# Two of the four sums of weight blocks in the seven-product stage made by accumulating loads that GpSimd issues

## The chip, the cores and the metric

The kernel runs on one core of a Trainium2 chip. The metric is the device time of one execution in microseconds (us); the number quoted is the median of the runs shown. In views of the trace PE is TensorE, with its weight loads apart as PEld; DVE is VectorE, ACT is ScalarE, POOL is GpSimd, and SP is the engine that issues every DMA (a transfer between HBM, the chip's main memory, and the on-chip memory) of the kernel before.

## The reference, cut to what matters

Two layers of a transformer-like block run over 256 latent tokens and 256 context tokens. Everything is float32. The change lies in the first layer's feed-forward part, which both token streams go through with the same weights:

```python
def swiglu(h, w_up, w_down):
    gu = h @ w_up
    return (jax.nn.silu(gu[..., :FFN_HIDDEN]) * gu[..., FFN_HIDDEN:]) @ w_down
```

`h` has 1024 features and `FFN_HIDDEN` is 2816, so `w_up` has 22 pairs of column tiles of 128: a gate tile and an up tile each.

## The kernel before, in words

**A recorded plan.** The kernel does not issue its instructions as it is written. A recorder, `Plan`, collects all operations with the tiles that they read and write. `place` hands out buffers: tiles of one class share a fixed number of slots, given out in the order in which they came free. Class `raw` has 7 slots (4 KB for each of 128 partitions) and takes weights as they come from HBM, and sums of them; `whi` and `wlo` have 3 slots each. `order` then runs a list scheduler with a cost for each operation (`cost`), a latency for each engine, and a port that certain VectorE and GpSimd operations share (`shares`); `emit` issues the operations in that order, so every row of the trace has the line of `emit`, 313. Each engine then works through its own queue in order, and waits at an instruction whose inputs are not there.

**Split matmuls.** A float32 product is made of three float32r matmuls. A weight tile is split first: ScalarE rounds it into `hi` (`whi<-raw`), VectorE subtracts that from the original into `lo` (`wlo<-raw,whi`). The three products are hi*hi, hi*lo and lo*hi.

**The seven-product stage.** For 19 of the 22 hidden tiles of the first layer (j = 3 to 21), `up_seven` replaces the eight block products of a two-by-two block product (two halves of the 1024 features by gate and up) with seven, after Strassen and Winograd. A weight pair is four blocks of 128 x 512: b11 (gate, first half of the features), b21 (gate, second half), b12 (up, first half) and b22 (up, second half). The seven products use as weights b11 (called f1), b22 (f3), b21 (f2) and four sums:

```python
t1 = b11 + b12      t2 = t1 + b22      t3 = b12 + b22      t4 = t2 + b21
```

A call of `up_seven` loads two tiles of 512 KB, `raw[0]` = (b11, b22) and `raw[1]` = (b12, b21), and makes the sums on VectorE into two more `raw` tiles, `y` = (t1, t2) and `z` = (t3, t4), called `upy` and `upz` in the trace. Three tiles of 128 x 1024 are split: (f1, f3), (t1, t2), (t3, t4), and `f2` apart into a tile `wf`. Then TensorE runs the products in the order f1, t1, t2, f3, t3, f2, t4. Each is 12 matmuls of 256 columns, 84 in a call. Their right sides are tokens (`h` in the trace) or sums of tokens made earlier (`hs0` to `hs3`), so a row `up<-hs0h,whi` belongs to t1, `hs1` to t2, `hs2` to f3, `hs3` to t3, and `h,wf` to f2. The results gather in three PSUM banks (a, b, c) that are read between products:

```python
product(a, "f1", block(0, 0), True)
nc.scalar.activation(e[:, 0], a, AF.Copy)
product(c, "t1", sums[0], True)
nc.scalar.activation(f[:, 0], c, AF.Copy)
product(a, "t2", sums[1], False)
nc.scalar.activation(e[:, 1], a, AF.Copy)
product(c, "f3", sums[2], False)
```

So product t2, which adds to bank a, cannot start before ScalarE has copied a (`upe<-up`); t3 waits in the same way for the second copy. A tanh (`upf<-upe`, then `upe<-up`), two multiplications and a write to `hid` end a call. Between calls, `ada_step` puts in tiles of the conditioning vectors: a load `raw<-in_w_ada_t` and one or two passes `junkv<-raw,silb` on VectorE; in this stage one in every second call.

**What stands around the stage.** Ahead of it are the output projection (`pj`), two layer norms for each stream, whose inverse roots are taken by GpSimd (`rsp`, `rsn`, an instruction with `pow`), and the first three hidden tiles by eight products (`up_tile`). Behind it is the projection with `w_down` (`pj` again).

Of the kernel before, what the change touches and what calls it, by code (L numbers as in the profile page):

```python
# [10 lines left out]
F32 = mybir.dt.float32  # L11
F32R = mybir.dt.float32r
BF16 = mybir.dt.bfloat16
AF = mybir.ActivationFunctionType
ALU = mybir.AluOpType
# [114 lines left out]
class Plan:  # L130
# [29 lines left out]
    def cost(self, eng, method, args, kw, outs, ins):  # L160

        src = ins[0] if ins else outs[0]
        n = max(v.idx.size for v in (outs[0:1] or ins[0:1]))
        if eng == "tensor":
            if method == "transpose":
                return 0.109
            if kw["rhs"].tile.dt == F32R:
                return max(n, 256) * 0.4434e-3 + 0.0045
            return max(4 * n / 2400, 0.214)
        if eng == "scalar":  # L170
            c = src.idx.size / 1200 + (0.05 if src.tile.cls == "bank" else 0.093)
            c += 0.18 if isinstance(kw.get("scale"), View) else 0
            return c + (0.093 if kw.get("accum_out") is not None else 0)
        if eng == "vector":
            n = max(v.idx.size for v in (*outs[:1], *ins))
            wide = [v for v in ins if v.idx.size > 8]
            fast = (method in ("tensor_scalar", "tensor_copy") and len(wide) == 1
                    and wide[0].tile.cls != "bank")
            return n / (1920 if fast else 960) + 0.07
        if eng == "gpsimd":  # L180
            return n / 440 + 0.1 if n > 64 else 0.4 + 0.19 * max(0, n - 1)
        return max(0.35, 128 * n * 4 / 365e3)

    @staticmethod
    def shares(eng, ins):

        return eng == "gpsimd" or eng == "vector" and sum(v.tile.cls not in ("bank", "dram") for v in ins) >= 2

    def place(self):

# [45 lines left out]
    def order(self):  # L236
        n = len(self.ops)
# [14 lines left out]
        out = []  # L252
        port = 0.0
        warm, busy = False, 0.0
        while len(out) < n:
            best = None
            for e in self.ENGINES:
                t = clock[e]
                if not avail[e]:
                    if not future[e]:  # L260
                        continue
                    t = max(t, future[e][0][0])
                if best is None or t < best[0]:
                    best = (t, e)
            t, e = best
            while future[e] and future[e][0][0] <= t:
                heapq.heappush(avail[e], heapq.heappop(future[e])[1:])
            rank, i = avail[e][0]
# [17 lines left out]
            if self.shares(e, self.ops[i][5]):  # L286
                t = max(t, port)
# [3 lines left out]
            out.append(i)  # L291
            for u in users[i]:
                lat = 0.0 if self.ops[u][0] == e == "tensor" else self.LATENCY[e]
                if self.ops[u][0] == "tensor" and e != "tensor":
                    lat += 0.12
                ready[u] = max(ready[u], t + c + lat)
                waits[u] -= 1
                if not waits[u]:
                    heapq.heappush(future[self.ops[u][0]], (ready[u], self.rank[u], u))
# [25 lines left out]
class Builder:  # L325
# [681 lines left out]
    def up_seven(self, j, hT, S, dst):  # L1007

        nc, io = self.nc, self.io
        raw = [self.nc.tile("raw", [128, 2, 4, 128], F32, "raw") for _ in range(2)]  # L1010
        for i in range(2):
            nc.sync.dma_start(raw[i], io["w_up7"][j, i])
        f1, f3, b12, f2 = raw[0][:, 0], raw[0][:, 1], raw[1][:, 0], raw[1][:, 1]
        y = self.nc.tile("raw", [128, 2, 4, 128], F32, "upy")
        z = self.nc.tile("raw", [128, 2, 4, 128], F32, "upz")
        w = {}

        def part(src, names):
            hi = self.nc.tile("whi", [128, 2, 4, 128], F32R, "whi")
            lo = self.nc.tile("wlo", [128, 2, 4, 128], F32R, "wlo")  # L1020
            self.split_sbuf(HL(hi, lo), src)
            for i, n in enumerate(names):
                w[n] = HL(hi[:, i], lo[:, i])

        part(raw[0], ("f1", "f3"))
        nc.vector.tensor_tensor(y[:, 0], f1, b12, op=ALU.add)
        nc.vector.tensor_tensor(y[:, 1], y[:, 0], f3, op=ALU.add)
        part(y, ("t1", "t2"))
        nc.vector.tensor_tensor(z[:, 0], b12, f3, op=ALU.add)
        nc.vector.tensor_tensor(z[:, 1], y[:, 1], f2, op=ALU.add)  # L1030
        part(z, ("t3", "t4"))
        wf = self.a_tile([128, 2, 4, 128], F32R, "wf2")
        w["f2"] = HL(wf[:, 0], wf[:, 1])
        self.split_sbuf(w["f2"], f2)

        def block(kh, half):
            c = slice(half * 128, half * 128 + 128)
# [9 lines left out]
        e = self.s_tile([128, 2, 2, 128], "upe")  # L1047
# [430 lines left out]
def lay_out(inputs):  # L1478
# [3 lines left out]
    out = {}  # L1482
# [26 lines left out]
    up = g["w_up"].reshape(L, KD, 128, 2, KF, 128)  # L1509
    out["w_up"] = up.transpose(0, 4, 3, 2, 1, 5)  # L1510
    q = out["w_up"][0].reshape(KF, 2, 128, 2, 4, 128)
    out["w_up7"] = np.stack([np.stack([q[:, 0, :, 0], q[:, 1, :, 1]], axis=2),
                             np.stack([q[:, 1, :, 0], q[:, 0, :, 1]], axis=2)], axis=1)
    tok = g["w_up"][1].reshape(4, 2, 128, 2, FH)[..., :512]
    out["w_up_tok"] = tok.transpose(3, 0, 2, 1, 4)
    out["w_down"] = g["w_down"].reshape(L, KF, 128, D)
# [7 lines left out]
    t = np.arange(SEQ)  # L1524
    ph = lambda k: 2 * np.pi * ((t[:, None] * k[None, :]) % 256) / 256
    f1 = np.concatenate([np.cos(ph(np.arange(129))), np.sin(ph(np.arange(1, 128)))], axis=1)
# [34 lines left out]
```

## Time and profile before

| | |
|---|---|
| median of 3 runs | 1322.76 us (1322.4 to 1326.71) |
| the profiled execution | 1323.69 us |
| its span, first to last instruction | 1321.9 us |
| TensorE's granted clock, mean | 0.993 of full speed |
| TensorE busy | 1297.4 us, 98% |
| VectorE busy | 1000.4 us, 76% |
| ScalarE busy | 660.9 us, 50% |
| GpSimd busy | 102.4 us, 8% |
| moved by DMA | 214.27 MB, 162 GB/s over the span |

A busy TensorE is not TensorE at its peak: matmuls are pipelined, a row of the trace lasts longer than the distance to the next, and so distances between matmuls, not their durations, tell its pace. Stages are best read one by one, by windows of the span (in us from its start). Releasers of a wait are inferred from semaphores (counters by which one engine tells another that it is done).

### The profile page before, as it was taken

The numbers are of one execution on the slowest core, as the hardware profiler recorded it, in microseconds if no ns is written. First come the engines' busy times: TensorE is split into PE (matmuls) and PEld (weight loads), VectorE is DVE, ScalarE is ACT, GpSimd is POOL, SyncE is SP. The second block draws the span as 40 slices with busy tenths as digits, with TensorE's granted clock in tenths as the row PEclk, the third lists the DMA queues.
The fourth block names the chain that finished last, engine by engine and source line by source line (L and its number), as shares of the span: only waits on it lengthen the run. The fifth ranks groups of instructions, "written<-read, shape, count | busy, mean of one in ns | idle before, by whom it ended". The sixth has DMA issues, their size and how long they took to land.

```text
span 1321.9 us, 20368 instructions
## 1 busy us (share of the span) xinstructions
PE 1297.4 (98%) x7846; PEld 1145.6 (87%) x7846; DVE 1000.4 (76%) x1774; ACT 660.9 (50%) x1192; POOL 102.4 (8%) x99
## 2 busy tenths in 40 slices
PE   9999999999999999999999999989999999999997
PEld 8887888788888889999999888868789998799985
DVE  6988996675764787799999994677777758666665
ACT  4656675332222347555555433575865544544450
POOL 1032100000010111000000000142000101000000
PEclk8999999999999999999999999999999999999999
DMA  9633334344543840233435896043245874465551
GB/s 367 224 105 117 114 108 159 113 131 155 175 159 129 303 159 27 71 127 114 158 107 171 288 343 206 26 127 128 83 137 184 278 263 161 168 192 183 186 190 48
DMA packets 60817, 214.27 MB, mean 162 GB/s; under 512 B 7296, under 2 KB 8112, under 8 KB 60720
## 3 DMA queue, kind: packets, MB, share of 16 engines
q1 hardware_dynamic: 60720, 212.98, 47.9%
q8 instruction: 61, 1.00, 0.3%
q14 instruction: 36, 0.29, 0.1%
HBM read 211.88 MB, written 1.07 MB: 161 GB/s over the span
## 4 chain that ended last, share of the span: by engine, by line
PE 81%; DVE 11%; ACT 5%; issue 2%; POOL 1%; DMA 0%; SPq 0%; DVEq 0%; ACTq 0%; POOLq 0%
PE up L313 25%; PE pj L313 17%; PE gp L313 15%; PE bp L313 10%; PE zp L313 8%; DVE junkv L313 2%; ACT prob L313 2%; DVE wlo L313 1%; DVE mx L313 1%; PE ut L313 1%; ACT junka L313 1%; PE pvp L313 1%; DVE ptl L313 1%; DVE y L313 1%; DVE bst L313 1%
## 5 line engine op out<-in xcount | busy, mean ns | idle before, releaser
L313 DVE TENSOR_TENSOR wlo<-raw,whi 128x1024 fp32r<-128x1024 f32 x216 | 265.3, 1229 | 122.8 <-ACT whi L313 121.5
L313 ACT ACTIVATE whi<-raw 128x1024 fp32r<-128x1024 f32 x216 | 228.2, 1058 | 193.7 <-PE bp L313 71.3
L313 DVE SCALAR_TENSOR_TENSOR junkv<-raw,silb 128x1024 bf16<-128x1024 f32 x128 | 156.7, 1224 | 12.0 <-DMA raw<-in_w_ada_t 10.6
L313 PE MATMUL up<-h,whi 128*128 128x256 f32 x880 | 157.5, 281 | 0.0
L313 PEld LDWEIGHTS up<-h,whi 128*128 128x128 f32 x880 | 135.3, 189 | 0.1
L313 PE MATMUL up<-h,wlo 128*128 128x256 f32 x440 | 123.7, 281 | 0.0
L313 PE MATMUL gp<-hT,whi 128*128 128x512 f32 x384 | 121.0, 395 | 0.0
L313 PE MATMUL zp<-whi,hT 128*128 128x512 f32 x320 | 113.5, 406 | 0.6 <-DVE u L313 0.4
L313 PEld LDWEIGHTS gp<-hT,whi 128*128 128x128 f32 x384 | 71.1, 188 | 15.1
L313 PEld LDWEIGHTS up<-h,wlo 128*128 128x128 f32 x440 | 83.1, 189 | 0.0
L313 PE MATMUL pj<-whi,hidp 128*128 128x512 f32 x256 | 79.9, 392 | 0.0
L313 ACT ACTIVATE gth<-gp 128x512 f32<-128x512 f32 (+1 forms) x48 | 23.5, 490 | 104.5 <-PE gp L313 104.3
L313 PE MATMUL gp<-hT,wlo 128*128 128x512 f32 x192 | 75.5, 393 | 0.0
L313 PEld LDWEIGHTS zp<-whi,hT 128*128 128x128 f32 x320 | 60.6, 191 | 13.8 <-DVE u L313 0.7
L313 PE MATMUL gp<-hx,whi 128*128 128x256 f32 x384 | 70.4, 284 | 0.0
L313 PE MATMUL zp<-whi,hx 128*128 128x512 f32 x192 | 66.0, 404 | 0.6 <-ACT hc L313 0.6
L313 DVE TENSOR_TENSOR rlo<-raw,rhi 128x1024 fp32r<-128x1024 f32 x44 | 54.9, 1258 | 12.6 <-ACT rhi L313 12.4
L313 PE MATMUL zp<-wlo,hT 128*128 128x512 f32 x160 | 63.8, 400 | 0.1
L313 PE MATMUL bp<-aT,whi 128*128 128x512 f32 (+1 forms) x256 | 63.0, 336 | 0.0
L313 POOL TENSOR_TENSOR gth<-gth 128x512 f32<-128x512 f32 (+1 forms) x16 | 27.9, 1745 | 444.9 <-DVE gth L313 274.9
L313 PEld LDWEIGHTS gp<-hx,whi 128*128 128x128 f32 x384 | 59.6, 190 | 0.2
L313 ACT ACTIVATE rhi<-raw 128x1024 fp32r<-128x1024 f32 x44 | 46.0, 1056 | 24.9 <-DMA raw<-in_w_down 15.6
(292 smaller groups left out, 3228.4 us busy)
## 6 DMA issues: line engine op xcount, KB each, us to landing
raw<-in_w_ada_t SPq DMA_DIRECT2D x80, 512.0 KB, 4.2
raw<-in_w_up SPq DMA_DIRECT2D x80, 512.0 KB, 3.9
raw<-in_w_in_tok SPq DMA_DIRECT2D x48, 512.0 KB, 4.2
raw<-in_w_gate SPq DMA_DIRECT2D x48, 512.0 KB, 3.7
raw<-in_w_down SPq DMA_DIRECT2D x44, 512.0 KB, 4.2
raw<-in_w_br SPq DMA_DIRECT2D x32, 512.0 KB, 3.6
raw<-in_w_out SPq DMA_DIRECT2D x19, 512.0 KB, 5.4
wsc<-in_w_ada_t SPq DMA_DIRECT2D x8, 512.0 KB, 10.3
```

What stands on the lines that cost most here:

```text
L313: getattr(getattr(nc, eng), method)(*map(real, args), **{k: real(a) for k, a in kw.items()})
```

## The change

The host lays the weights out anew: `w_up7` has three pairs of blocks, (b11, b22), (b11, b12) and (b12, b22), and b21 stands alone as `w_up7f`. A call of `up_seven` loads (b11, b22) into `raw`, (b11, b12) into a `raw` tile called `upt`, and b21 into `half` (256 KB). A DMA issued by GpSimd with `accum_op=add` then adds (b12, b22) to `upt` as it lands, which makes t1 and t3. VectorE makes t2 and t4 from them into a tile `upu`. Since t1 and t2 now lie in different tiles, the four sums are split one by one, in blocks of 128 x 512. The scheduler is told the cost and latency of such a DMA, and that an operation of GpSimd with one input or none does not use the shared port.

```diff
+        if method == "dma_start" and eng == "gpsimd":
+            return 1.1
...
-        return eng == "gpsimd" or eng == "vector" and sum(v.tile.cls not in ("bank", "dram") for v in ins) >= 2
+        return eng == "gpsimd" and len(ins) > 1 or eng == "vector" and sum(v.tile.cls not in ("bank", "dram") for v in ins) >= 2
...
+                if self.ops[i][1] == "dma_start" and e == "gpsimd":
+                    lat = 4.5
...
-        raw = [self.nc.tile("raw", [128, 2, 4, 128], F32, "raw") for _ in range(2)]
-        for i in range(2):
-            nc.sync.dma_start(raw[i], io["w_up7"][j, i])
-        f1, f3, b12, f2 = raw[0][:, 0], raw[0][:, 1], raw[1][:, 0], raw[1][:, 1]
-        y = self.nc.tile("raw", [128, 2, 4, 128], F32, "upy")
-        z = self.nc.tile("raw", [128, 2, 4, 128], F32, "upz")
+        raw = self.nc.tile("raw", [128, 2, 4, 128], F32, "raw")
+        nc.sync.dma_start(raw, io["w_up7"][j, 0])
+        t = self.nc.tile("raw", [128, 2, 4, 128], F32, "upt")
+        nc.sync.dma_start(t, io["w_up7"][j, 1])
+        nc.gpsimd.dma_start(t, io["w_up7"][j, 2], accum_op=ALU.add)
+        half = self.nc.tile("raw", [128, 4, 128], F32, "raw")
+        nc.sync.dma_start(half, io["w_up7f"][j])
+        u = self.nc.tile("raw", [128, 2, 4, 128], F32, "upu")
+        f1, f3, t1, t3, t2, t4 = raw[:, 0], raw[:, 1], t[:, 0], t[:, 1], u[:, 0], u[:, 1]
...
-        part(raw[0], ("f1", "f3"))
-        nc.vector.tensor_tensor(y[:, 0], f1, b12, op=ALU.add)
-        nc.vector.tensor_tensor(y[:, 1], y[:, 0], f3, op=ALU.add)
-        part(y, ("t1", "t2"))
-        nc.vector.tensor_tensor(z[:, 0], b12, f3, op=ALU.add)
-        nc.vector.tensor_tensor(z[:, 1], y[:, 1], f2, op=ALU.add)
-        part(z, ("t3", "t4"))
+        part(pair(), [raw], ("f1", "f3"))
+        nc.vector.tensor_tensor(t2, t1, f3, op=ALU.add)
+        part(pair(), [t1, t2], ("t1", "t2"))
+        nc.vector.tensor_tensor(t4, t2, half, op=ALU.add)
+        part(pair(), [t3, t4], ("t3", "t4"))
...
-        self.split_sbuf(w["f2"], f2)
+        self.split_sbuf(w["f2"], half)
```

ScalarE's queue before, one call from the middle of the stage (`wf` is f2 of a later call, `upe<-up` the copies of bank a and one half of the tanh, `upf<-upe` the other half):

```order
L313 ACTIVATE whi<-raw 128x1024
L313 ACTIVATE whi<-upy 128x1024
L313 ACTIVATE wf_5631<-raw 128x512
L313 ACTIVATE upf<-upe 128x256
L313 ACTIVATE whi<-upz 128x1024
L313 ACTIVATE upe<-up 128x256 x2
L313 ACTIVATE upf<-up 128x256
L313 ACTIVATE upe<-up 128x256
L313 ACTIVATE whi<-raw 128x1024
```

and the same engine now:

```order
L317 ACTIVATE whi<-upt 128x512
L317 ACTIVATE whi<-upu 128x512
L317 ACTIVATE upe<-up 128x256
L317 ACTIVATE wf_5680<-raw 128x512
L317 ACTIVATE upe<-up 128x256
L317 ACTIVATE upf<-up 128x256
L317 ACTIVATE wf_5717<-raw 128x512
L317 ACTIVATE upe<-up 128x256
L317 ACTIVATE whi<-raw 128x1024
```

The splits of `wf` moved: they come two in every second call, one directly ahead of the first copy of bank a (behind the two splits of t3 and t4), the other directly ahead of the second. This group of nine rows comes seven times, with the next call's rows between.

GpSimd's queue before, from the last gate additions ahead of the layer norms:

```order
L313 TENSOR_TENSOR gth<-gth 128x512 x8
L313 TENSOR_TENSOR rsp<-ssp,mhalf 128x1
L313 TENSOR_TENSOR rsn<-ssn,mhalf 128x1
L313 TENSOR_TENSOR rsp<-ssp,mhalf 128x1
L313 TENSOR_TENSOR rsn<-ssn,mhalf 128x1
L313 TENSOR_TENSOR rsp<-ssp,mhalf 128x1 x2
L313 TENSOR_TENSOR rsn<-ssn,mhalf 128x1 x2
```

and now:

```order
L317 TENSOR_TENSOR gth<-gth 128x512 x8
L317 DMA upt<-in_w_up 128x1024 x2
L317 TENSOR_TENSOR rsp<-ssp,mhalf 128x1
L317 TENSOR_TENSOR rsn<-ssn,mhalf 128x1
L317 TENSOR_TENSOR rsp<-ssp,mhalf 128x1
L317 TENSOR_TENSOR rsn<-ssn,mhalf 128x1
L317 TENSOR_TENSOR rsp<-ssp,mhalf 128x1 x2
L317 TENSOR_TENSOR rsn<-ssn,mhalf 128x1 x2
L317 DMA upt<-in_w_up 128x1024 x17
```

The first two accumulating loads stand ahead of the layer norms' roots; the other 17 have GpSimd to themselves.

SP's queue before, two calls in the middle of the stage:

```order
L313 DMA raw<-in_w_ada_t 128x1024
L313 DMA raw<-in_w_up 128x1024 x4
L313 DMA raw<-in_w_ada_t 128x1024
L313 DMA raw<-in_w_up 128x1024 x4
L313 DMA raw<-in_w_ada_t 128x1024
```

and now (`upt` is the plain load of (b11, b12), `in_w_up7f` the half; the name of `w_up7` is printed as `in_w_up`):

```order
L317 DMA raw<-in_w_ada_t 128x1024
L317 DMA raw<-in_w_up 128x1024
L317 DMA raw<-in_w_up7f 128x512 x2
L317 DMA raw<-in_w_up 128x1024
L317 DMA upt<-in_w_up 128x1024 x2
L317 DMA raw<-in_w_ada_t 128x1024
```

Two calls have seven loads on SP where they had five, the two halves next to each other. The first of the pair goes into the slot of a (b11, b22) and so waits for its split, the second into the slot of the conditioning tile and waits for the pass over that. A call's `upt` takes the slot in which the half of two calls ago lay, which is last read by the sum t4 of that call; only the last two calls take theirs from a `upu`, which is last read by the split of t4.

## Rows read from the trace of the kernel before

**Rows 1.** The profile page, the chain of work that ended last, by engine and by line.

```profile
PE 81%; DVE 11%; ACT 5%; issue 2%; POOL 1%; DMA 0%; SPq 0%; DVEq 0%; ACTq 0%; POOLq 0%
```

**Rows 2.** The same chain in order of time, from the output projection to the end of the projection with `w_down`, and the plain feed-forward stage of the second layer: start, length, what, how many instructions.

```profile
507.13 17.02 PE up L313 x144
524.15 1.75 PE trp L313 x16
525.90 207.06 PE up L313 x1740
732.96 113.09 PE pj L313 x491
...
1149.96 1.79 PE up L313 x15
1152.18 100.24 PE up L313 x849
```

**Rows 3.** Busy time of each engine by windows of the span: window, its length, busy us and instructions of PE, PEld, DVE, ACT, POOL, then granted clock, DMA share and GB/s.

```profile
586.00:606.00 20.00, 20.00 (x170) 20.00 (x169) 19.03 (x33) 10.97 (x18) 0.00 (x0) 1.00 0.39 133
606.00:626.00 20.00, 20.00 (x171) 20.00 (x170) 18.91 (x33) 10.80 (x18) 0.00 (x0) 1.00 0.40 133
733.00:847.00 114.00, 114.00 (x498) 92.90 (x497) 86.32 (x133) 36.79 (x46) 3.69 (x4) 1.00 0.65 222
```

**Rows 4.** Instructions by tile: shortest, median and longest duration in ns, first and last start in us.

```profile
L313 ACT ACTIVATE upf<-up x19: 364/385/387, 546.3 to 726.3; 128x256 f32<-128x256 f32 x19
...
L313 DVE TENSOR_TENSOR upy<-raw x19: 683/685/687, 492.2 to 712.1; 128x512 f32<-128x512 f32 x19
L313 DVE TENSOR_TENSOR upy<-upy,raw x19: 683/685/689, 494.0 to 713.1; 128x512 f32<-128x512 f32 x19
L313 DVE TENSOR_TENSOR upz<-upy,raw x19: 681/684/687, 495.2 to 716.4; 128x512 f32<-128x512 f32 x19
L313 ACT ACTIVATE whi<-upy x19: 1047/1061/1156, 508.2 to 718.6; 128x1024 fp32r<-128x1024 f32 x19
L313 DVE TENSOR_TENSOR wlo<-upy,whi x19: 1217/1219/1221, 522.2 to 720.6; 128x1024 fp32r<-128x1024 f32 x19
...
L313 DVE TENSOR_TENSOR upz<-raw x19: 682/684/689, 494.6 to 714.3; 128x512 f32<-128x512 f32 x19
L313 ACT ACTIVATE whi<-upz x19: 1049/1056/1065, 510.7 to 723.0; 128x1024 fp32r<-128x1024 f32 x19
L313 DVE TENSOR_TENSOR wlo<-upz,whi x19: 1215/1219/1221, 523.3 to 725.1; 128x1024 fp32r<-128x1024 f32 x19
...
L313 ACT ACTIVATE wf<-raw x19: 615/632/637, 516.9 to 710.4; 128x512 fp32r<-128x512 f32 x19
L313 DVE TENSOR_TENSOR wf<-raw,wf x19: 682/685/691, 524.8 to 717.0; 128x512 fp32r<-128x512 f32 x19
```

**Rows 5.** Instructions in order of time in one call in the middle of the stage, PE, ACT, DVE and SP: start, duration, engine, operation, and in brackets the idle time before it with its releaser.

```profile
603.14 0.40 PE L313 MATMUL up<-h,whi 128*128 128x256 f32 x2
604.57 0.28 PE L313 MATMUL up<-hs0h,whi 128*128 128x256 f32 x1
606.01 0.28 PE L313 MATMUL up<-hs1h,whi 128*128 128x256 f32 x1
...
605.64 1.22 DVE L313 TENSOR_TENSOR wlo<-upz,whi 128x1024 fp32r<-128x1024 f32 x1
606.93 0.88 SPq L313 DMA_DIRECT2D raw<-in_w_up  x2
607.63 0.39 ACT L313 ACTIVATE upe<-up 128x256 f32<-128x256 f32 x1 [1.04 <-PE up L313]
607.91 1.05 ACT L313 ACTIVATE whi<-raw 128x1024 fp32r<-128x1024 f32 x1
609.46 1.22 DVE L313 TENSOR_TENSOR wlo<-raw,whi 128x1024 fp32r<-128x1024 f32 x1
```

**Rows 6.** Loads: by source, size, and median us from issue to landing; of the whole span, then of the window 560 to 640 (the stage), then of 733 to 847 (the projection with `w_down`).

```profile
sgurow<-in_sgu_ln SPq DMA_DIRECT2D x4, 256.0 KB, 3.4
ropecs<-in_rope SPq DMA_DIRECT2D x2, 256.0 KB, 3.3
...
raw<-in_w_up SPq DMA_DIRECT2D x16, 512.0 KB, 4.2
...
raw<-in_w_down SPq DMA_DIRECT2D x18, 512.0 KB, 5.2
```

**Rows 7.** Who waited for whom between 526 and 733 us: total, times, longest.

```profile
ACT wf L313 <- DMA raw<-in_w_up: 14.7, 9, 2.3
```

**Rows 8.** Instructions in order of time ahead of the stage: two of SP's loads for it, GpSimd's first root, and what follows them.

```profile
474.62 0.33 SPq L313 DMA_DIRECT2D raw<-in_w_up  x1
479.84 0.33 SPq L313 DMA_DIRECT2D raw<-in_w_up  x1
484.52 1.52 POOL L313 TENSOR_TENSOR rsp<-ssp,mhalf 128x1 f32<-128x1 f32 x1 [23.08 <-DVE ssp L313]
486.70 1.28 DVE L313 SCALAR_TENSOR_TENSOR res<-y,rsp,lnrow 128x1024 f32<-128x1024 f32 x1
497.10 1.25 ACT L313 ACTIVATE y<-res,nb_n,rsn 128x1024 f32<-128x1024 f32 x1 [1.05 <-DVE nb_n L313]
499.62 1.03 PE L313 MATMUL trp<-idn,y 128*128 128x128 f32 x8
```

More of the change, by code (lines that the diff above doesn't have):

```diff
@@ L1016, in up_seven, with pair @@
+        t = self.nc.tile("raw", [128, 2, 4, 128], F32, "upt")
[5 more added lines that the diff above has]
+        f1, f3, t1, t3, t2, t4 = raw[:, 0], raw[:, 1], t[:, 0], t[:, 1], u[:, 0], u[:, 1]
         w = {}
[L1018 to L1021, printed above, removed]
+        def pair():
+            return (self.nc.tile("whi", [128, 2, 4, 128], F32R, "whi"), self.nc.tile("wlo", [128, 2, 4, 128], F32R, "wlo"))
@@ L1022, in part @@
+        def part(p, srcs, names):
+            hi, lo = p
             for i, n in enumerate(names):
                 w[n] = HL(hi[:, i], lo[:, i])
-        part(raw[0], ("f1", "f3"))
-        nc.vector.tensor_tensor(y[:, 0], f1, b12, op=ALU.add)
-        nc.vector.tensor_tensor(y[:, 1], y[:, 0], f3, op=ALU.add)
-        part(y, ("t1", "t2"))
-        nc.vector.tensor_tensor(z[:, 0], b12, f3, op=ALU.add)
-        nc.vector.tensor_tensor(z[:, 1], y[:, 1], f2, op=ALU.add)
-        part(z, ("t3", "t4"))
+                if len(srcs) > 1:
+                    self.split_sbuf(w[n], srcs[i])
+            if len(srcs) == 1:
+                self.split_sbuf(HL(hi, lo), srcs[0])
@@ L1511, in lay_out @@
     q = out["w_up"][0].reshape(KF, 2, 128, 2, 4, 128)
-    out["w_up7"] = np.stack([np.stack([q[:, 0, :, 0], q[:, 1, :, 1]], axis=2),
-                             np.stack([q[:, 1, :, 0], q[:, 0, :, 1]], axis=2)], axis=1)
+    b11, b21, b12, b22 = q[:, 0, :, 0], q[:, 0, :, 1], q[:, 1, :, 0], q[:, 1, :, 1]
+    out["w_up7"] = np.stack([np.stack(p, axis=2) for p in ((b11, b22), (b11, b12), (b12, b22))], axis=1)
+    out["w_up7f"] = b21
     tok = g["w_up"][1].reshape(4, 2, 128, 2, FH)[..., :512]
```

## The prediction

> **What bounds the kernel now.** I read the chain of work that ended last first. TensorE makes 81% of it [rows 1], and in order of time the whole of the changed stage is one piece of it: 1740 matmuls in 207.06 us from 525.90, with the projection with `w_down` right behind [rows 2]. Nothing else stands in the chain between 507 and 846 us. The windows say the same: TensorE is busy in 20.00 of 20.00 us, its clock granted in full, while VectorE is busy in 18.9 to 19.0 of them [rows 3]. So there are two engines near their limit, VectorE at 95% and TensorE at 100%. A row of 280 ns that starts every 120 ns would hide small gaps, so I check the pace: `upf<-up` occurs once a call, 19 times from 546.3 to 726.3 [rows 4], hence 180.0 / 18 = 10.00 us a call, and with 84 matmuls 0.1190 us each. The plain stage of the second layer, with the same 256 columns, takes 864 matmuls in 102.46 us (1149.96 to 1252.42), 0.1186 us each [rows 2]. At that pace a call is 9.96 us. So TensorE leaves at most 0.04 x 19 = 0.8 us to be won in the whole stage. That it waits for nobody is the fact on which the forecast rests.
>
> **The change part by part.** *VectorE.* Removed in a call: four sums (685 + 685 + 684 + 684 ns) and the `lo` of two tiles (2 x 1219), 5.18 us. Added: two sums (2 x 685) and four `lo` of half the width, for which `wf` with its 685 ns is the same form, 4.11 us [rows 4]. That is 1.07 us less in a call and 20 us in 19, from about 9.5 of 10 us to 8.4. *ScalarE.* Removed 1061 + 1056 ns, added 4 x 632 [rows 4]: 0.41 us more in a call, 7.8 us in all, from 5.4 of 10 us to 5.8. Neither is on the chain, so the 20 us come to nothing as long as TensorE paces the stage, and VectorE's freed time has no use downstream: the next stage is TensorE's too, with VectorE at 86.32 of 114 us [rows 3].
>
> *DMA.* A call loaded 1.05 MB and now moves 1.84 MB (three of 0.524, one of 0.262). At 133 GB/s the stage moves 1.33 MB in a call [rows 3]; with 0.79 more it is about 211 GB/s. The `w_down` stage moves 222 GB/s and TensorE does not wait there [rows 3], so the bytes alone cost nothing; but a load of 512 KB takes 5.2 us to land there and 4.2 in the stage now [rows 6].
>
> *The accumulating load itself.* No row shows one. From below it costs GpSimd and the DMA what a plain load of its size costs, 4.2 us [rows 6]; from above twice that, since it reads its target too, plus an issue like the root's 1.52 us [rows 8], 10 us. What covers it is the distance between the load of `upt` and its first reader, the sum t2. In the middle of the stage `upt` takes the slot of a half that the sum t4 read two calls ago; t2 and t4 of one call stand one to two us apart on VectorE, so the distance is 20 - 2 = 18 us. Less 4.2 for the plain load, 13.8 remain: even 10 us are hidden. In the last two calls the slot is freed by the split of t4 instead. That ends 3.7 us into its call (606.86 against f1 at 603.14 [rows 5]), and the sum t2 of two calls later stands about as deep in the call ahead of its own: one call, 10 us, of which 6 remain. Behind the waiting sum VectorE has the subtractions that read banks a and c, with about 2 us of room (0.9 to the end of f3, and a product of 1.4 ahead of t4), so only above 8 us does TensorE wait: at most 2 x 2 = 4 us. I take 5 to 6 us, nearer to the plain load, and so nothing.
>
> A rule of the Trainium skill speaks against such loads. What rows show: VectorE is busy 95% of the stage, with `tensor_tensor` in every row of it that stands here [rows 3, 4]. The page "SBUF — State Buffer", in its box on VectorE blocking DMA, says that GpSimd cannot write the descriptors of a DMA while VectorE runs an operation in a two-port mode, and lists copies and `tensor_scalar` as such, but no `tensor_tensor`. By that list the stage would have hardly any; if it held for all VectorE work, the third rival below would decide. No run shown here tells which.
>
> *GpSimd's queue.* The first two accumulating loads stand ahead of the roots of the layer norms. The second waits for an `upt` whose slot was filled at 479.84 before; it lands 4.2 us later, at 484.0, and GpSimd's first root starts at 484.52 [rows 8]. An issue of 1 to 2 us moves the root by 0.5 to 1.6 us, and its reader on VectorE (486.70, while the root ended at 486.04) by 0 to 0.9. The end of this chain is `y`, done at 498.35, for the transposes at 499.62 [rows 8], over 1 us later: hidden, one time.
>
> *ScalarE's order.* This is the place that I trust least. Seven times a split of `wf` now stands directly ahead of the copy that frees bank a for product t2, and one ahead of the copy for t3. Take T = 603.14, where f1 begins [rows 5], and 613.14 for the next call. The split of (f1, f3) ends on VectorE at 609.46 + 1.22 = 610.68, or T - 2.46; SP issues 0.07 us behind such a split (606.86 and 606.93) [rows 5], so the first half leaves at T - 2.4. ScalarE must begin its split in time for t2, which starts at T + 2.87 (606.01): less the copy (0.39) and the split (0.63, some 0.1 of it overlapped, as 607.63 + 0.39 against the next at 607.91), that is T + 1.9 [rows 4, 5]. So the half has 4.3 us to land. A load of 256 KB takes 3.3 or 3.4 us where it is seen [rows 6]: 0.9 us to spare. In the same stretch ScalarE has two splits and a tanh behind t4. A product is seen to have ended 0.2 us into the next (the copy behind t2 starts at 607.63, and t2, from 606.01, takes 10.00 / 7 = 1.43), so ScalarE is free at T + 0.2 + 0.53 + 0.53 + 0.3 = T + 1.6 at the earliest, 0.3 us to spare. The second half, by the same steps, leaves behind the conditioning pass at about T + 0.5 and has some 4.1 us. Upper end: both as slow as the 512 KB of the `w_down` stage, 5.2 us [rows 6], 0.9 and 1.1 us late, and 7 x 2.0 = 14 us in all. ScalarE waited 14.7 us for such halves before, 9 times [rows 7], at no cost, but there a copy of bank a did not stand behind them. I take 3.4 to 4 us, and no wait.
>
> Sum: span 1321.9 + 0 for the DMA, + 0 to 0.5 for GpSimd's queue, - 0 to 0.8 of pace. The profiled execution took 1323.69 us, 1.8 above its span and 0.9 above the median. So the median of the runs stays: 1322.76 + about 0.2, **1323.0 us**.
>
> **The rivals.** *Slower: the halves come late.* The accumulating load starts near T - 4.5 (its `upt` leaves behind a sum t4, about T - 9, and takes 4.2) and is still moving when the first half leaves at T - 2.4. If it slows the half by more than 0.9 us, ScalarE stands at the split with the copy of bank a behind it, TensorE stops ahead of t2, and a stage without slack never makes it up. Price 0 to 14 us, from 4.3 us of landing on; at 4.8 us for both about 8, or 1331. For it: the tight places above, and a load that reads and writes. Against: DMA engines are busy 40% of the stage [rows 3].
>
> *Faster: VectorE was the true limit.* Then 20 us less of VectorE would shorten the stage by up to 20, to 1303. For it: 95% busy. Against: TensorE's pace is within 0.3% of that of a stage in which VectorE has time to spare, and no wait of TensorE is in the chain [rows 2].
>
> *Slower: VectorE holds GpSimd off.* If GpSimd could issue only in gaps of VectorE, an issue would wait up to most of a call, 8 to 10 us, on top of the 5 to 6. Just over the 13.8 us of the middle, and far over the 8 of the last two calls: 2 x 8 = 16 us there and a few in the middle, 1342.
>
> **How the numbers follow.** No change, 0.76 (with it the case that single waits cost up to 4 us). Halves late by enough to be seen, 0.16. VectorE holding GpSimd off, 0.04. VectorE as the limit, 0.04. Some 0.3%, 4 us, is what a measurement here can tell from no change. So faster 0.04, within 0.3% 0.76, slower 0.16 + 0.04 = 0.20. The likeliest case alone spans 1321 to 1327 (the runs before went up to 1326.71). The range takes in the halves' rival up to its middle price: 1320 to 1331.
>
> **What would show it.** Right: 19 calls at 10.0 us, read from the rows of `upf<-up`; VectorE near 8.4 of 10 us in the stage, with the idle time put down to TensorE; the sum t2 never idle for `upt` in the middle. Wrong: a period over 10.1 us, with idle time of ScalarE ahead of `wf` put down to a DMA and TensorE waiting for `upe`; VectorE idle ahead of `upu` for a DMA from GpSimd; or the stretch between 484 and 500 us longer, with TensorE waiting at its transposes. A period under 9.95 us would say that the stage was not TensorE's.

## The result and the profile after

The changed kernel takes 1337.57 us (median of 4 runs, 1336.57 to 1340.32); the kernel before took 1322.58 us beside it (4 runs, 1322.12 to 1326.71). The ratio is 1.0105, 95% interval 1.009 to 1.012: 15 us slower, above the range of the prediction. The profiled execution took 1338.06 us with a span of 1336.3 us, 14.4 more than the span before.

I read the views in the same order as before; the line of `emit`, which every row carries, is now 317 (in the experiments 313, 317, 319 or 338). First the chain of work that ended last, by engine on the profile's page [rows 1]:

```profile
PE 76%; DVE 12%; ACT 6%; DMA 3%; issue 2%; POOL 1%; DVEq 0%; ACTq 0%; POOLq 0%
```

TensorE has lost 5 of its 81 parts in a hundred, and a DMA stands in the chain with 3%. In order of time, in the stage [rows 2]: start, length, what, how many.

```profile
526.65 33.24 PE up L317 x275
...
560.42 1.13 DVE wlo L317
561.58 4.65 DMA raw<-in_w_up7f
566.25 0.63 ACT wf L317
566.88 0.28 ACT upe L317
567.20 13.07 PE up L317 x108
...
603.34 7.28 DMA raw<-in_w_up7f
...
611.60 13.08 PE up L317 x108
...
690.75 6.70 DMA raw<-in_w_up7f
...
698.42 48.78 PE up L317 x396
```

One piece of 207.06 us has fallen into eight, and between each two lies the same sequence: a split on VectorE sets a `raw` slot free, the load of b21 (`in_w_up7f`, the half) runs 4.65 to 7.28 us, ScalarE splits it into `wf`, ScalarE copies bank a, TensorE goes on. Seven such legs of DMA, with a median of 5.89 us, stand in the chain (a leg is the time from a load's issue to its landing).

Who waited for whom between 526 and 740 us says the same [rows 7]: total, times, longest.

```profile
ACT wf L317 <- DMA raw<-in_w_up7f: 14.9, 8, 3.3
...
PE up L317 <- ACT upe L317: 10.1, 7, 2.8
...
DVE upu L317 <- DMA upt<-in_w_up: 1.5, 2, 1.2
```

ScalarE's wait for f2 is no longer than before (14.7 us then), but now TensorE waits 10.1 us behind it, where before it waited for nobody. The sum t2 waited for an accumulating load only twice, for 1.5 us.

One stall in order of time [rows 5], from POOL, SP, ACT and PE: start, duration, operation, in brackets the idle time before it.

```profile
602.77 0.87 POOL L317 DMA_DIRECT2D upt<-in_w_up  x1 [7.31 <-ACT whi L317]
603.34 3.34 SPq L317 DMA_DIRECT2D raw<-in_w_up7f  x2
...
610.64 0.63 ACT L317 ACTIVATE wf<-raw 128x512 fp32r<-128x512 f32 x1 [3.29 <-DMA raw<-in_w_up7f]
611.18 0.36 ACT L317 ACTIVATE upe<-up 128x256 f32<-128x256 f32 x1
...
611.60 0.39 PE L317 MATMUL up<-hs1h,whi 128*128 128x256 f32 x1 [2.77 <-ACT upe L317]
```

`hs1h` is the first right side of t2: ScalarE stands at the split, the copy of bank a that t2 needs stands behind it. All seven stalls are ahead of t2, so it is the first half of each pair that stops TensorE, not the second (ScalarE waited once for a second half, 1.16 us at 677.36, and TensorE did not wait behind that). The room can be read from them: landing less stall is 7.28 - 2.77 = 4.51 us here and 6.70 - 2.23 = 4.47 at the last one (TensorE's row at 698.42), and in all seven it lies between 4.47 and 4.51. The neighbour is there each time: in all seven an accumulating load was issued 0.1 to 2.5 us ahead of the first half (here at 602.77), and such a load takes 5.6 us to land.

Windows [rows 3] and tiles [rows 4]: busy us and instructions of PE, PEld, DVE, ACT, POOL, then granted clock, DMA share, GB/s; and shortest, median, longest ns with first and last start.

```profile
586.00:606.00 20.00, 18.83 (x158) 18.62 (x157) 15.39 (x29) 9.70 (x20) 1.75 (x2) 1.00 0.69 190
606.00:626.00 20.00, 17.23 (x145) 17.02 (x144) 13.79 (x28) 10.56 (x21) 1.72 (x2) 1.00 0.71 198
...
694.00:698.00 4.00, 2.19 (x19) 1.99 (x17) 2.88 (x7) 1.25 (x3) 0.00 (x0) 1.00 0.83 225
698.00:702.00 4.00, 3.58 (x18) 3.58 (x19) 2.14 (x5) 2.10 (x6) 0.00 (x0) 0.61 0.46 145
...
L317 ACT ACTIVATE upf<-up x19: 364/383/386, 547.1 to 740.6; 128x256 f32<-128x256 f32 x19
...
L317 POOL DMA_DIRECT2D upt<-in_w_up x19: 862/874/1066, 481.6 to 724.9; - x19
```

The 18 periods of `upf<-up` take 193.5 us, 13.5 more than the 180.0 before. Of these 10.1 are the stalls themselves. Six of the pieces behind a stall take 13.06 to 13.11 us for 108 matmuls, 0.23 more than 108 x 0.119, 1.4 in six. Idle time is counted from the end of a row, and a row lasts 0.28 us where the next starts 0.12 after it: so 0.16 of the 0.23 is time lost at the stall that its idle time does not hold; what the rest is, was not tried. The last, 396 matmuls in 48.78 us, lost 1.7, most of it in the clock, granted at 0.61 on the mean of the 4 us window behind that stall. Together 13.2.

Loads [rows 6], over the whole span: the two queues (packets, MB, share of 16 engines' span), then the loads with their median us to landing.

```profile
q1 hardware_dynamic: 63456, 217.96, 49.2%
q0 software_dynamic: 2736, 9.96, 4.5%
...
upt<-in_w_up SPq DMA_DIRECT2D x19, 512.0 KB, 4.3
upt<-in_w_up POOLq DMA_DIRECT2D x19, 512.0 KB, 5.6
raw<-in_w_up7f SPq DMA_DIRECT2D x19, 256.0 KB, 5.2
```

The median of a row is taken over those loads whose landing the trace holds, five of the 19 halves here (4.14 to 6.70 us). q0 holds the accumulating loads: a packet takes 0.045 x 16 x 1336.3 / 2736 = 0.35 us, against 0.492 x 16 x 1336.3 / 63456 = 0.17 in q1. So a stage that moves 1.4 to 1.5 times the bytes (190 and 198 GB/s against 133) keeps the DMA engines busy 1.8 times as long (0.69 to 0.71 against 0.39 to 0.40).

### The profile page after: what moved, and what is told of

Same layout as the page of the kernel before. It is cut to its first block, busy times and chain, and to the rows that moved or that the text cites. A ratio compares the mean times of both kernels' runs of the same rounds, so it can differ in the third digit from the quotient of the medians.

```text
span 1336.3 us, 20568 instructions
## 1 busy us (share of the span) xinstructions
PE 1301.2 (97%) x7846; PEld 1148.6 (86%) x7846; DVE 981.0 (73%) x1774; ACT 663.0 (50%) x1230; POOL 118.2 (9%) x118
## 3 DMA queue, kind: packets, MB, share of 16 engines
q1 hardware_dynamic: 63456, 217.96, 49.2%
q0 software_dynamic: 2736, 9.96, 4.5%
HBM read 226.82 MB, written 1.07 MB: 171 GB/s over the span
## 4 chain that ended last, share of the span: by engine, by line
PE 76%; DVE 12%; ACT 6%; DMA 3%; issue 2%; POOL 1%; DVEq 0%; ACTq 0%; POOLq 0%
PE up L317 20%; PE pj L317 17%; PE gp L317 15%; PE bp L317 10%; PE zp L317 8%; DMA raw<-in_w_up7f 3%; DVE junkv L317 2%; DVE wlo L317 2%; ACT prob L317 2%; PE ut L317 1%; DVE mx L317 1%; ACT junka L317 1%; DVE y L317 1%; PE pvp L317 1%; DVE ptl L317 1%
## 5 line engine op out<-in xcount | busy, mean ns | idle before, releaser
L317 ACT ACTIVATE rhi<-raw 128x1024 fp32r<-128x1024 f32 x44 | 45.8, 1055 | 24.6 <-DMA raw<-in_w_down 20.8
```

The lines of the kernel that those rows point to most:

```text
L317: getattr(getattr(nc, eng), method)(*map(real, args), **{k: real(a) for k, a in kw.items()})
```

## The experiments

The theory that the profile suggests: the adding makes a load's packets twice as long; the half beside it lands later than the 4.5 us for which ScalarE's order has room; the copy of bank a behind it stops TensorE. Rivals: the bytes alone do it; an accumulating load slows TensorE wherever the half is split; the new order of the queues does it, without a late load; VectorE's work still matters. The ratios with their intervals are taken from all runs of both kernels, so they are not exactly the ratio of the two medians.

**1. The splits of `wf` behind the copies.** A pass behind the scheduler moves each split of `wf` on ScalarE behind the third copy, and its `lo` on VectorE with it; the queues of TensorE, GpSimd and SP stay.

```diff
-        return out
+        return self.behind(out)
+
+    def behind(self, out):
...
+            move = [w]
+            move += [i for i in out[k + 1:m] if w in self.deps[i]]
...
+            out = out[:k] + [i for i in out[k:m] if i not in move] + move + out[m:]
```

> The changed kernel with one thing moved: the splits of wf that stand ahead of the copies of banks a and c go behind the third copy, on ScalarE and with them their other half on VectorE; the queues of TensorE, GpSimd and SP are the same row for row. Theory (the half lands 1 to 3 us after the time by which ScalarE needs it, and the copy of bank a stands behind its split): the seven waits of TensorE for upe go, calls of 10.0 us, 1323 to 1326 us; the half itself still takes about 5 us to land. Rival (the accumulating loads, or GpSimd's issuing, hold the stage up in another way, and the split only shows it): 1333 us or more, with the waits at other places. Second rival (ScalarE's smaller splits are what is too much): above 1330 too, with ScalarE busy at the waits.

Measured: 1330.00 us (4 runs, 1329.06 to 1333.07), ratio 1.0056 (1.0038 to 1.0074). Half of the loss went, where the theory had expected all of it (1323 to 1326). The waits of its stage:

```profile
DVE wf L338 <- ACT wf L338: 8.9, 10, 1.4
...
PE up L338 <- DVE upf L338: 4.2, 5, 1.7
```

No wait of TensorE for `upe` is left. In its place VectorE, in order like ScalarE, stands at the `lo` of the late half with the subtractions behind it that read the banks, and TensorE waits for those. The chain of this kernel still holds five legs of the half (5.01 to 6.27 us). So the theory's place was right, and the edit moved part of the wait to the next queue. (A sixth leg, of 6.89 us, is an accumulating load for one of the last calls; the wait of TensorE behind it took 0.72.)

**2. The same loads without adding.** GpSimd's load is a plain one, so b12 and b22 stand where the sums t1 and t3 should. ScalarE and VectorE go through the stage in the order of the changed kernel.

```diff
-        nc.gpsimd.dma_start(t, io["w_up7"][j, 2], accum_op=ALU.add)
+        nc.gpsimd.dma_start(t, io["w_up7"][j, 2])
```

> All queues as in the changed kernel, but GpSimd's load does not accumulate: it overwrites, so that b12 and b22 stand where t1 and t3 should, and the output is that of other weights. The bytes that come from HBM, the issuing engine and the places of all instructions stay. If the adding is what makes the neighbouring half slow (its packets took 0.35 us each against 0.17 of plain ones), the half lands in 3.5 to 4.3 us and most of the seven waits go: 1323 to 1328 us. If the bytes and the place in the queue alone do it, the half still takes about 5 us: 1333 to 1338 us.

Measured: 1325.34 us (10 runs, 1322.93 to 1329.23), ratio 1.0017 (1.0006 to 1.0028). Its loads, its waits and one of its windows:

```profile
q0 software_dynamic: 2736, 9.96, 2.4%
...
upt<-in_w_up POOLq DMA_DIRECT2D x19, 512.0 KB, 4.0
raw<-in_w_up7f SPq DMA_DIRECT2D x19, 256.0 KB, 4.3
...
PE up L317 <- ACT upe L317: 1.7, 2, 1.1
...
606.00:626.00 20.00, 20.00 (x171) 20.00 (x170) 16.73 (x33) 10.93 (x22) 1.05 (x2) 1.00 0.62 211
```

The same order and as many bytes (211 GB/s) cost 2.5 us, and 12 of the 15 are gone. A packet of q0 takes 0.024 x 16 x 1327.4 / 2736 = 0.19 us. The half lands in 4.3 us at the median, just inside the room of 4.5, and two stalls remain. They confirm the room: their halves land in 5.12 and 5.54 us and TensorE stands 0.65 and 1.08, a difference of 4.47 and 4.46. (The profiled execution, 1329.23 us, is the slowest of the ten.)

**3. A small accumulating load.** Adding stays, on 16 of 128 partitions (64 KB), so t1 and t3 are sums there alone; the order of the stage stays as well.

```diff
-        nc.gpsimd.dma_start(t, io["w_up7"][j, 2], accum_op=ALU.add)
+        nc.gpsimd.dma_start(t[0:16], io["w_up7"][j, 2][0:16], accum_op=ALU.add)
```

> All queues as in the changed kernel, but GpSimd's load adds on 16 of the 128 partitions only, 64 KB in place of 512, so t1 and t3 are sums there alone. If the traffic of the accumulating load is what delays the half: landing at 3.4 to 4 us, no waits, 1322 to 1325 us. If the half is late for what SP itself has loading (two calls' tiles in a bunch) or for its place in the queue: landing above 4.3 us and 1330 us or more.

Measured: 1325.09 us (10 runs, 1324.32 to 1325.51), ratio 1.0013 (1.0004 to 1.0022).

```profile
raw<-in_w_up7f SPq DMA_DIRECT2D x19, 256.0 KB, 2.8
...
L317 ACT ACTIVATE upf<-up x19: 368/385/389, 546.1 to 726.1; 128x256 f32<-128x256 f32 x19
```

The half lands in 2.8 us, sooner than the 3.4 to 4 expected, TensorE waits for no split of it, and the 18 periods are 180.0 us as before. The five halves whose landing is known leave at the same places of the queue in all three kernels: 4.14 to 6.70 us in the changed one, 2.73 to 5.54 with plain loads, 2.70 to 2.85 here. The 2 us of the median above the kernel before are not lost in the stage: the chains of both traces end at 1318.7 and 1318.8 us. GpSimd issues as many loads as in the changed kernel. So neither their issue nor the new order costs this time; what the loads do to the DMA engines does.

**4. The kernel before with two sums less on VectorE.** The sums t3 and t4 are left out, and their products take the blocks as loaded: 1.37 us less VectorE in a call, and no load more or less. The scheduler orders the rest anew.

```diff
-        z = self.nc.tile("raw", [128, 2, 4, 128], F32, "upz")
...
-        nc.vector.tensor_tensor(z[:, 0], b12, f3, op=ALU.add)
-        nc.vector.tensor_tensor(z[:, 1], y[:, 1], f2, op=ALU.add)
-        part(z, ("t3", "t4"))
+        part(raw[1], ("t3", "t4"))
```

> The kernel before without the sums t3 and t4: their products take b12 and b21 as they were loaded, so the output is that of other weights. VectorE has 1.37 us less to do in each of 19 calls, 26 us, more than the change takes from it, and nothing is added. Theory (TensorE paces the stage): 1321 to 1324 us, calls of 10.0 us. Rival (VectorE, 95% busy, is the limit): about 10 to 26 us less, 1297 to 1313 us.

Measured: 1324.84 us (10 runs, 1323.56 to 1325.89), ratio 1.0013 (1.0003 to 1.0023), no gain.

```profile
L313 ACT ACTIVATE upf<-up x19: 383/384/386, 546.2 to 726.4; 128x256 f32<-128x256 f32 x19
...
606.00:626.00 20.00, 20.00 (x171) 20.00 (x170) 16.14 (x26) 10.67 (x18) 0.00 (x0) 1.00 0.35 106
```

VectorE has 16.14 of 20 us where it had 18.91, and the period stays 10.0 us. So the rival that VectorE is the limit is out: less work for it gains nothing.

**5 and 6. The scheduler told how long the half takes.** It counted 2.6 us for any load of SP on top of the time of its bytes (`cost`, 0.72 us for a half), so 3.3 us from issue to landing. One number is added, 5.0 us in the one kernel and 7.0 in the other in place of the 2.6, so 5.7 and 7.7 in all; the work is the same.

```diff
+                if e == "sync" and self.ops[i][4] and self.ops[i][4][0].tile.full == [128, 4, 128]:
+                    lat = 7.0
```

> The changed kernel with one number added: the scheduler is told that the load of the half (128 x 512) takes 5.0 us to land, where it counted 2.6 for every load of SP. The same work, but its order changes by itself: only one split of wf in two calls still stands directly ahead of a copy of bank a on ScalarE, the other stands ahead of the tanh; a half leaves SP earlier against its split. Main theory (halves that land in 5 to 6 us stand in the way of the copies): about half of the loss goes, 1328 to 1332, with fewer waits of TensorE for upe. Rival (any accumulating load beside the stage costs its time, wherever the split of wf stands): 1336 to 1338, as the changed kernel. Rival (an order of the queues alone, without a late half, costs the time): no number follows, but the losses would not stand at waits for the half.

> The changed kernel with the scheduler told 7.0 us for the landing of the half. No split of wf stands directly ahead of a copy of bank a any more: on ScalarE they stand behind the third copy and ahead of the tanh, and the lo of wf on VectorE stands later too. Main theory: a half that lands in 5 to 6 us is then no longer in anyone's way, 1322 to 1327, 10.0 us a call by the rows of upf, and no wait of TensorE for upe; with more than 2 us of waits of TensorE for VectorE it falls short as the kernel with wf behind the copies did (1330). Rival (accumulating loads cost time in any order): 1334 to 1338.

Measured: 1329.31 us with 5.0 (5 runs, 1328.37 to 1330.93), ratio 1.0035 (1.0021 to 1.0049), and 1327.25 us with 7.0 (9 runs, 1324.10 to 1330.24), ratio 1.0025 (1.0012 to 1.0038); the kernel before took 1323.43 us beside them. With 5.0 the time is in the range expected, though by another way than I had it: the half's legs are gone from the chain, and three legs of the accumulating load (`upt`, 6.44 to 7.50 us) stand there instead. With 7.0 it is just above the range expected (1322 to 1327). Of the kernel with 7.0, two windows of the middle and the window at the end, and VectorE's two waits in the latter:

```profile
586.00:606.00 20.00, 20.00 (x170) 20.00 (x170) 16.90 (x33) 11.09 (x22) 1.96 (x3) 1.00 0.80 219
606.00:626.00 20.00, 20.00 (x170) 20.00 (x170) 16.82 (x33) 11.09 (x22) 1.73 (x2) 1.00 0.76 208
...
706.00:726.00 20.00, 18.50 (x156) 18.30 (x156) 15.98 (x29) 8.95 (x18) 0.89 (x1) 1.00 0.84 254
...
707.80 0.69 DVE L319 TENSOR_TENSOR upu<-upt,raw 128x512 f32<-128x512 f32 x1 [1.61 <-DMA upt<-in_w_up]
...
719.17 0.69 DVE L319 TENSOR_TENSOR upu<-upt,raw 128x512 f32<-128x512 f32 x1 [1.94 <-DMA upt<-in_w_up]
```

From 546 to 706 us TensorE is busy in all windows, with one accumulating load in each call and the DMA engines busy 0.76 to 0.80 in these two. Within the stage the loss is in the last two calls, where the sum t2 waits for `upt` and TensorE loses 1.5 us. Of the 4.0 us by which its span is longer, 2.2 are there at the end of the projection with `w_down` (848.29 us against 846.05). Of the other 1.8, 1.6 arise in the 50 us behind that, up to the next long piece of the chain (898.69 us against 894.86): TensorE's clock is granted there at 0.90 and 0.93 in the windows 868 to 888, where before it had 1.00 in 866 to 886. Why it fell there is open; the stretch lies behind the changed stage, and the changed kernel itself takes 48.8 us for it.

**7. The half in another buffer.** It takes a slot of class A and needs no `raw` slot, so that the scheduler could load it earlier.

```diff
-        half = self.nc.tile("raw", [128, 4, 128], F32, "raw")
+        half = self.a_tile([128, 4, 128], F32, "half")
```

> The changed kernel with the half loaded into a buffer of another class, so that its load needs not wait for a raw slot and can leave SP much earlier than its split; the order of the whole stage changes by itself, and five raw tiles a call are four. Main theory (the half comes late because it leaves late and lands slowly): 1322 to 1327, the waits of ScalarE for the half gone. Rival (the accumulating loads themselves cost TensorE or the engines' ports time): 1334 to 1338. A time between them would have to be read from the waits.

Measured: 1332.36 us (4 runs, 1331.07 to 1334.18), ratio 1.006 (1.0043 to 1.0076): between the two, so the waits decide. Between 526 and 747 us:

```profile
ACT wf L317 <- DMA half<-in_w_up7f: 13.3, 7, 4.7
...
PE up L317 <- ACT upf L317: 5.2, 3, 3.2
```

The waits of ScalarE for the half are not gone, against the expectation; TensorE now stands ahead of f3, for the copy of bank c behind the split. The chain has three legs of the half, of 7.92, 5.03 and 6.34 us. The scheduler still counted 3.3 us for them, and I take it that it placed some as tightly as before with its new freedom; that was not tried by itself. The other buffer gave back 5 of the 15 us.

**8. The kernel before with accumulating loads nobody reads.** The loads follow only each other. The scheduler's lines of the change come with them (not shown).

```diff
...
+        if j == 3:
+            self.extra = self.a_tile([128, 2, 4, 128], F32, "extra")
+            nc.sync.dma_start(self.extra, io["w_up7"][j, 1])
+        nc.gpsimd.dma_start(self.extra, io["w_up7"][j, 1], accum_op=ALU.add)
```

> The kernel before, with 19 accumulating loads of 512 KB by GpSimd added whose target nobody reads; VectorE still makes all four sums. They depend only on each other, so they run back to back from about 495 us, over roughly the first half of the stage, more densely than one in a call. Main theory (accumulating traffic slows its neighbours' landing, and only an order without room turns that into time): loads of 512 KB land in 5 to 7 us instead of 4.2 while it lasts; the kernel before had waits of ScalarE for f2 without a copy behind them, so 1322 to 1327. Rival (accumulating loads cost TensorE's pace by themselves, through ports or bandwidth): 0.7 us for each, as in the changed kernel (13.5 / 19), 1334 to 1338, and a period of upf above 10.1 us exactly while the loads run.

Measured: 1342.37 us (4 runs, 1340.06 to 1349.23), ratio 1.0143 (1.011 to 1.0176), above the ranges of both the theory and the rival. It is partly a fault of the experiment. The buffer `extra` is given on to a row of a later layer norm, and SP's queue shows it:

```profile
624.44 0.93 SPq L317 DMA_DIRECT2D raw<-in_w_up  x2
646.26 0.33 SPq L317 DMA_DIRECT2D lnrow<-in_ln  x1
646.69 0.85 SPq L317 DMA_DIRECT2D raw<-in_w_up  x2
```

SP stood 20.8 us for the last of the 19 loads, and TensorE then waited 11.3 us in one piece. Without that piece 7 to 8 us remain. Four shorter waits of TensorE for a copy of bank a make 4.2 of them; behind the long one the clock is granted at 0.50 and then 0.71 for two windows of 4 us, which costs some 2 us more (40 matmuls where 57 fit). So here too the loss stands at such waits, but the run was not clean enough to decide.

**9. Latency 7.0, and the last two calls summed by VectorE.** For j = 20 and 21 a plain load of (b12, b22) and four sums in place; 17 calls keep the accumulating load.

```diff
...
+        plain = j >= 20
-        nc.sync.dma_start(t, io["w_up7"][j, 1])
-        nc.gpsimd.dma_start(t, io["w_up7"][j, 2], accum_op=ALU.add)
+        nc.sync.dma_start(t, io["w_up7"][j, 2 if plain else 1])
+        if not plain:
+            nc.gpsimd.dma_start(t, io["w_up7"][j, 2], accum_op=ALU.add)
...
+        if plain:
+            nc.vector.tensor_tensor(t3, t1, f3, op=ALU.add)
+            nc.vector.tensor_tensor(t1, f1, t1, op=ALU.add)
```

> The kernel with the landing of the half counted as 7.0 us (1327.25), in which the last two calls (j = 20 and 21) make all four sums on VectorE from a plain load of (b12, b22), in place; 17 calls keep their accumulating load. In the former, TensorE was busy in 20.00 of 20 us from 546 to 706 us and lost its time between 706 and 726, where VectorE waited 1.6 and 1.9 us for the last two upt. Main theory (accumulating loads cost nothing where the order leaves them and the halves room, and the rest of the loss is the last two calls): those waits go, 1322 to 1325, upf from call to call 10.0 us throughout. Rival (accumulating loads cost some pace everywhere): 1326 to 1328, as before the edit.

Measured: 1324.36 us (11 runs, 1323.37 to 1324.65) against 1323.34 (15 runs, 1322.53 to 1326.95), ratio 1.000 (0.9991 to 1.0009). Tiles, the last piece of its chain in the stage, and its loads between 526 and 720 us:

```profile
L319 ACT ACTIVATE upf<-up x19: 365/385/387, 546.5 to 726.5; 128x256 f32<-128x256 f32 x19
...
526.13 207.04 PE up L319 x1739
...
upt<-in_w_up POOLq DMA_DIRECT2D x15, 512.0 KB, 7.6
...
raw<-in_w_up7f SPq DMA_DIRECT2D x16, 256.0 KB, 6.4
```

The halves land in 6.4 us and the accumulating loads in 7.6, later than in the changed kernel, and nothing is lost: 180.0 us, one piece of 207.04. So the accumulating load by itself costs TensorE nothing, to within the 0.1% of the interval; it costs time where the order has no room for the loads beside it. No version beat the kernel before, which fits experiment 4: VectorE's freed time has no taker.

**10. Experiment 8 mended.** One accumulating load a call into a buffer of its own class, behind a copy of one column of the call's t2 on GpSimd.

```diff
...
+        nc.gpsimd.tensor_copy(self.extra[:, 0, 0, 0:1], y[:, 1, 0, 0:1])
+        nc.gpsimd.dma_start(self.extra, io["w_up7"][j, 1], accum_op=ALU.add)
```

> The kernel before, with one accumulating load of 512 KB a call into a buffer of its own that nobody reads; a copy of one column from the call's t2 on GpSimd ahead of it sets the pace. It mends the former experiment of that kind, in which the loads ran back to back and their buffer held up a load of SP behind it at 646 us. VectorE still makes all four sums. Main theory (one accumulating load a call costs only what the order of the rest has no room for): the kernel before has more room for its loads, so 0 to 4 us, 1322 to 1327, with waits of ScalarE for f2 longer than 14.7 us in all. Rival (accumulating loads cost TensorE's pace by themselves): 10 us or more, 1333 and up.

Measured: 1335.53 us (4 runs, 1333.91 to 1336.56), ratio 1.0084 (1.0069 to 1.0099). The number is the rival's, yet the rows are the theory's: its waits, its loads, its tile.

```profile
ACT wf L317 <- DMA raw<-in_w_up: 39.1, 14, 4.9
...
PE up L317 <- ACT upe L317: 5.5, 7, 1.8
...
raw<-in_w_up SPq DMA_DIRECT2D x33, 512.0 KB, 6.0
...
L317 ACT ACTIVATE upf<-up x19: 364/384/387, 547.3 to 737.0; 128x256 f32<-128x256 f32 x19
```

The loads of `w_up7` land in 6.0 us instead of 4.2, ScalarE waits 39.1 us for f2 instead of 14.7, and TensorE stands behind it for a copy of bank a, as in the changed kernel. Since experiment 9 has an accumulating load in 17 calls, with slower landings, and no loss, it is again the order that has no room, this time that of the kernel before: in the stage ScalarE and VectorE go through the same rows in the same order. Of the 9.7 us by which the 18 periods are longer, 5.5 are these seven waits; 0.2 lost besides at each, and a clock granted at 0.50 from 666 to 668 us, behind the longest of them, make some 2.5 more; the rest is open. My expectation that it had more was wrong; ScalarE's waits of 14.7 us [rows 7] were a sign of that which I did not read.

## Why the prediction was wrong

**What bounds the kernel**: right. TensorE paces the stage. Experiment 4 took 26 us from VectorE (19 x 1.37), experiment 9 some 18 (17 x 1.07), and the period stayed at 10.0 us.

**VectorE and ScalarE**: right in size. In the undisturbed order of experiment 6 VectorE has 16.8 to 16.9 of 20 us, 8.4 of 10 as forecast, and ScalarE 11.09 of 20, 5.5 of 10 against 5.8 (the rows of two splits in a row overlap by 0.1 us).

**DMA**: the bytes were estimated well (211 GB/s; experiment 2 moved 211), and "the bytes alone cost nothing" holds but for 2.5 us at most (experiments 3 and 4 lie 2 us above the kernel before as well, without a loss in the stage). What I left out is that an accumulating packet takes twice as long. The share of the engines that I set against the rival, 40%, was that of the stage before: the bytes alone make it 62% (experiment 2), and with the adding it is 69 to 71% although fewer bytes move in a microsecond.

**The accumulating load itself**: right. Taken 5 to 6 us, measured 5.6; hidden in the middle; 1.5 us of waits in the last two calls, which cost TensorE nothing there; in experiment 6, where the load lands later, VectorE waits 3.5 us and TensorE 1.5, inside the forecast 4.

**GpSimd's queue**: right. The stage starts at 526.65 instead of 525.90, of which 0.43 is there already at the output projection (461.53 against 461.10), so 0.3 us.

**VectorE holding GpSimd off**: did not happen. GpSimd's issue takes 0.87 us at the median and 1.07 at most, beside a VectorE that is busy 77% and 69% of the two windows above, with `tensor_tensor` for the most part. That agrees with the Trainium skill, page "SBUF — State Buffer", section "Who interferes with whom", by which `tensor_tensor` has no two-port mode. (The list of operations stands in that section, not in the box that I named.)

**ScalarE's order**: the step that failed. "I take 3.4 to 4 us, and no wait": the first half lands in 4.65 to 7.28 us, seven times out of seven beyond its room. The room itself was right (4.3 us forecast, 4.5 measured), and so was the mechanism, which stood there as the rival with 0.16. Mis-sized was the landing. I took it from loads of 256 KB outside the stage [rows 6], none of them beside an accumulating load, and of those six the trace holds only two landings (3.35 and 3.32 us); yet the prediction itself had worked out that the accumulating load is still moving when the half leaves. With that neighbour made light the half lands in 2.8 us, with a plain one in 4.3, with the adding one in 5.2. That the price came near my upper end, 13.5 against 14, is luck, for it came another way: only the first half is late, by 1.4 us on the mean, not both by 0.9 and 1.1, and each stall costs 0.2 us, and one a lower clock, on top. Since the term that I trusted least had so little room (0.9 us) and its size lay between 3.4 and 5.2 by my own rows, the range should have reached to the end of that price, 1337; the measured 1337.57 would still lie above that. The argument that before "a copy of bank a did not stand behind" the waits of 14.7 us did not hold either: the queue is in order, the copy stood a few rows further behind, and experiment 10 shows it reached.

## What to carry to other kernels

Cost a load in the time that it occupies the DMA engines, not in bytes, and cost its neighbours too: here a load that adds as it lands let the loads beside it land later. Before a landing is taken from a view, count the loads behind its median and see what moved beside them. Where an order is planned with one latency for all loads, a change of traffic uses up room that the plan never held; look in each in-order queue for the instruction that waits for a load and for what stands behind it, and tell the planner the landing that the trace shows. Before work is taken from an engine, ask whether the engine that paces the stage gets anything for it; here it got nothing, in any order.

## What the runs showed of the hardware that I had not expected

A packet of an accumulating load takes 0.35 us, of a plain load through the same queue 0.19, of SP's loads 0.17. The view of queues counts 9.96 MB for both kinds, 19 x 0.524, so a byte count does not tell them apart and only the time does. That it is the reading of the target which takes the time was not tried.

A half of 256 KB, in the same places of the same queues, lands at the median of five in 2.8, 4.3 or 5.2 us, by whether GpSimd's load beside it is small, plain or adding.

TensorE's clock fell after one of the seven stalls, and not the longest: after 2.23 us of idle time at 698.42 it was granted at 0.61 on the mean of 4 us, 0.50 from 699 to 702; after 2.77 us at 611.60 the rows to 626 show 1.00. In experiment 10 it fell after only 1.83 us of idle time (0.50 from 666 to 668), in experiment 7 after 3.23 us (0.50 from 584 to 586). In experiment 8, within 11.3 us of idle, it is at 0.50 too, the lower of its two levels (1.2 of 2.4 GHz), as this window of it shows:

```profile
650.00:654.00 4.00, 0.00 (x0) 0.00 (x0) 2.06 (x5) 0.94 (x2) 0.00 (x0) 0.50 0.90 356
```

So the length of the stall alone does not decide it; what does, stays open.
